# Router with stationary tokens, ranks by differences, and a transposed first gather, in a fused attention and mixture-of-experts block

## Chip, core and metric

One core of a Trainium2 chip. The metric is the device time of one execution in microseconds (us). Engines are named as the profile names them: PE (TensorE, with PEld for its weight loads), DVE (VectorE), ACT (ScalarE), POOL (GpSimd) and SP (SyncE, which here only issues DMAs). All data is 32-bit floating point unless said otherwise.

## What is computed

256 tokens of width 2048 pass a block with a spatial gating unit and a forgetting attention side by side, and then a mixture of 32 experts, of which each token uses two. Cut to the part that matters here:

```python
x = x + (g_sgu * y_sgu + g_fox * y_fox) @ w_out          # end of the first half
h2 = rms_norm(x, norm2_g)
g_logits = h2 @ w_rg + b_rg                              # 4 groups
e_logits = (h2 @ w_re + b_re).reshape(T, 4, 8)           # 8 experts in each
grp = argmax(g_logits); e_logits = e_logits[grp]         # one group a token
top_v, top_i = top_k(e_logits, 2)                        # two experts of it
w_top = softmax(top_v) * softmax(g_logits)[grp]
# each expert: y = (silu(xi @ w_g[e]) * (xi @ w_u[e])) @ w_d[e] on its tokens, added with the gate
```

## The kernel before

**First half.** The tokens lie as two blocks of 128 (`NT = 2`, index `tb`). Every product with a large weight goes through `half`: 8 k-tiles of weight come in by one DMA, ACT and DVE split them into a high and a low part (lines 237 and 238), and PE makes three products for each (lines 243 to 245). Between the k-tiles, `tick` runs steps of a queue of generators, `side`: small work of the chunk before is put into PE's order among the large products. The last chunks are the product with `w_out`, in five column ranges: three of 512 and two of 256.

**Router.** After each column range, `out_side` adds the result to `x1`, takes the squares for the norm (into `ss`), transposes `x1` by 128 x 128 pieces (line 646), copies two k-tiles out of PSUM with the norm weight `g2T` multiplied in (line 648), and multiplies with the router weight `wr` (line 655). There the weight is stationary (64 columns) and 256 tokens move; even and odd k-tiles gather in the two halves of the partitions of one tile, `r_ps`. After the last range `r_ps` is copied to SBUF by ACT, and two products with `fold` (two identities one over the other) add the halves and turn the result to tokens by 36 logits (`l_ps`, line 699). Line 706 scales by the norm and adds the bias. Then DVE finds the group (`first_max`), the eight logits of that group, and each expert's rank among the eight by comparing all pairs (lines 749 to 776). PE keeps busy meanwhile with `keep_warm(WARM[5])`, 60 small products that nobody reads. Five small products count each expert's tokens (`c_ps`), and `pos1` gives each token its slot.

**Experts.** An expert has 32 slots (`CAP`). `gather` picks its tokens from `x1` by products with a selection matrix `sel` (line 826: `sel` stationary, 512 columns of `x1` moving, four ranges side by side in the array), copies them (line 829), transposes (line 832) and scales by `g2p` (line 834) to `xT`. `hidden` multiplies `xT` with the gate or up weight (line 873); `silu`, `times_up` and `down` follow. While one expert is worked on, the next one's tokens are gathered.

**Expert weights** come in loads of 2 MB (12 MB for an expert) into tiles that are free by then: `order` and `free` give tiles to loads in turn, and line 561 issues them on SP's queue. Eleven tiles' worth are filled before the experts start: the last of these, `rb` and the second `mT`, may be overwritten only when the last product with `w_out` is done. After them no tile is free until the first expert's gate product has read the first one, `hT`.

The order on each engine is fixed when the program is built.

Of the kernel before, what the change touches and what calls it, by code (L numbers as in the profile page):

```python
# [9 lines left out]
F32 = mybir.dt.float32  # L10
# [4 lines left out]
ALU = mybir.AluOpType  # L15
AX = mybir.AxisListType

P = 128
# [15 lines left out]
HW = 2 * QW  # L34
CUTS = (0, 2, 4, 6, 8, 12, 16)
AHEADS = (2, 1, 1, 0, 1, 0, 1, 0, 0, 1, 0, 1, 1)
FRONT = ("g1T", "g2T", "wr", "fold", "br", "qkg", "bsT", "bfr", "mhalf", "eps_t", "ss", "rstd")
WARM = (45, 20, 0, 6, 4, 60, 0)
OVER_AT = 1
NEG = -1.0e30  # L40

# [2 lines left out]
def hybrid_block(ctx: ExitStack, tc: tile.TileContext, a, out, dbg=None):  # L44
# [11 lines left out]
    def ctile(shape, dt, name):  # L56
        return (fc if name in FRONT else cp).tile(shape, dt, tag=name, name=name)

# [2 lines left out]
    g2T = ctile([P, KT], F32, "g2T")  # L61
    g2p = ctile([P, 4, 4], F32, "g2p")
    wr = ctile([P, KT, 64], F32, "wr")
    fold = ctile([P, NG + NE], F32, "fold")
    br = ctile([P, NG + NE], F32, "br")
    qkg = ctile([P, 2], F32, "qkg")
    bsT = ctile([P, NH], F32, "bsT")
# [434 lines left out]
    zz = z_chunk(9)  # L502
    flush()
    load_small([(g2T, "g2T"), (wr, "wr"), (br, "br"), (g2p, "g2p")])
    side.append(evac_act(zz, va, AF.Copy, 512))
    side.append(attention_side(qT, kT, va))

# [116 lines left out]
        side.append(m_side(y2, t, n))  # L624

    r_ps = scp.tile([P, 512], F32, tag="sc", name="r_ps")[:, :S]

    def out_side(zz, b, c0, width):  # L630
        nk = width // P
        k0 = c0 // P
        for tb in range(NT):
            xs = x1[:, tb, c0:c0 + width]
            nc.vector.tensor_tensor(xs, xs, zz[tb], ALU.add)
        yield
        for tb in range(NT):
            xs = x1[:, tb, c0:c0 + width]
            sq = zt_tile()[:, :width]
            keep(nc.scalar.activation(sq, xs, AF.Square, accum_out=ss[:, tb, b:b + 1]))  # L640
        xTs = []
        for i in range(0, nk, 2):
            ps = tr_tile().rearrange("p (i t) q -> p i t q", i=2)
            for j in range(2):
                for tb in range(NT):
                    keep(nc.tensor.transpose(ps[:, j, tb], x1[:, tb, c0 + (i + j) * P:c0 + (i + j + 1) * P], ident))
            xT = zt_tile().rearrange("p (i t) -> p i t", i=2)
            nc.vector.tensor_tensor(xT, ps.rearrange("p i t q -> p i (t q)"),
                                    g2T[:, k0 + i:k0 + i + 2].unsqueeze(2).to_broadcast([P, 2, S]), ALU.mult)
            xTs.append(xT)  # L650
            yield
        for i, xT in enumerate(xTs):
            for j in range(2):
                kt = k0 + 2 * i + j
                keep(nc.tensor.matmul(r_ps[64 * j:64 * j + 64], wr[:, kt], xT[:, j], start=(kt < 2), stop=(kt >= KT - 2)))
            yield

    def w_out(c0, width, k):
# [28 lines left out]
    for z, b, c0 in parts:  # L687
        load(AHEADS[b + 8])
        half(z, w_out(c0, 256, 1), mT[1], start=False, width=256)
        flush()  # L690
        side.append(out_side(z, b, c0, 256))
    room([rings[used["ring"] % 2].rearrange("p a b -> p (a b)")])
    load(2)
    flush()
    rT = zt_tile()[:, :S]
    nc.scalar.activation(rT, r_ps, AF.Copy)
    l_ps = scp.tile([P, 512], F32, tag="sc", name="l_ps")[:, :NT * (NG + NE)].rearrange("p (t e) -> p t e", t=NT)
    for tb in range(NT):
        nc.tensor.matmul(l_ps[:, tb], rT[:, tb * P:(tb + 1) * P], fold, start=True, stop=True)
    s2 = small.tile([P, NT], F32, tag="s2", name="s2")  # L700
    nc.vector.tensor_reduce(s2, ss[:, :, :4], AX.X, ALU.add)
    nc.vector.tensor_scalar(s2, s2, 1.0 / D, EPS, ALU.mult, ALU.add)
    nc.vector.scalar_tensor_tensor(s2, ss[:, :, 4], 1.0 / D, s2, ALU.mult, ALU.add)
    rsqrt(rstd2, s2)
    for tb in range(NT):
        nc.vector.scalar_tensor_tensor(lg[:, tb], l_ps[:, tb], rstd2[:, tb:tb + 1], br, ALU.mult, ALU.add)
    front.close()
    if dbg is not None:
        nc.sync.dma_start(dbg[:, 0:2 * D], x1.rearrange("p a b -> p (a b)"))
# [23 lines left out]
    tt, ts, stt = nc.vector.tensor_tensor, nc.vector.tensor_scalar, nc.vector.scalar_tensor_tensor  # L733
    red = nc.vector.tensor_reduce

    def first_max(v, n, name):

        mx = rt([P, NT], name + "m")
        red(mx, v, AX.X, ALU.max)
        k = rt([P, NT, n], name + "k")  # L740
        tt(k, v, over(mx, n), ALU.is_equal)
        tt(k, k, desc[:, EPG - n:].unsqueeze(1).to_broadcast([P, NT, n]), ALU.mult)
        km = rt([P, NT], name + "km")
        red(km, k, AX.X, ALU.max)
        oh = rt([P, NT, n], name + "oh")
        tt(oh, k, over(km, n), ALU.is_equal)
        return mx, oh

    gl = lg[:, :, 0:NG]
    gm, goh = first_max(gl, NG, "g")  # L750
    gd = rt([P, NT, NG], "gd")
    tt(gd, gl, over(gm, NG), ALU.subtract)
    nc.scalar.activation(gd, gd, AF.Exp)
    pick = rt([P, NT, NG, EPG], "pick")
    goh4 = goh.unsqueeze(3).to_broadcast([P, NT, NG, EPG])
    tt(pick, lg[:, :, NG:].rearrange("p t (g e) -> p t g e", g=NG), goh4, ALU.mult)
    e8 = rt([P, NT, EPG], "e8")
    red(e8, pick.rearrange("p t g e -> p t e g"), AX.X, ALU.add)

    sq4 = [P, NT, EPG, EPG]  # L760
    bt = mo.tile(sq4, F32, tag="th", name="bt")
    be = mo.tile(sq4, F32, tag="h", name="be")
    ei = e8.unsqueeze(3).to_broadcast(sq4)
    ej = e8.unsqueeze(2).to_broadcast(sq4)
    tt(be, ej, ei, ALU.is_equal)
    tt(bt, ej, ei, ALU.is_gt)
    tt(be, be, low.unsqueeze(1).to_broadcast(sq4), ALU.mult)
    tt(bt, bt, be, ALU.add)
    rank = rt([P, NT, EPG], "rank")
    red(rank, bt, AX.X, ALU.add)  # L770
    oh12 = rt([P, NT, EPG], "oh12")
    ts(oh12, rank, 1.0, None, ALU.is_le)
    oo = rt([P, NT, NE], "oo")
    ob = rt([P, NT, NE], "ob", BF16)
    for o in (ob, oo):
        tt(o.rearrange("p t (g e) -> p t g e", g=NG), goh4, oh12.unsqueeze(2).to_broadcast([P, NT, NG, EPG]), ALU.mult)

    keep_warm(WARM[5])
    c_ps = scm.tile([P, 512], F32, tag="sc", name="c_ps")
# [12 lines left out]
    def gates():  # L792

        oh1 = rt([P, NT, EPG], "oh1")
        oh2 = rt([P, NT, EPG], "oh2")
        ts(oh1, rank, 0.0, None, ALU.is_equal)
        ts(oh2, rank, 1.0, None, ALU.is_equal)
        w1 = rt([P, NT], "w1")
        w2 = rt([P, NT], "w2")
        gs = rt([P, NT], "gs")  # L800
        red(gs, gd, AX.X, ALU.add)
        md = rt([P, NT, EPG], "md")
        tt(md, oh2, oh1, ALU.subtract)
        tt(md, md, e8, ALU.mult)
        red(w2, md, AX.X, ALU.add)
        nc.scalar.activation(w2, w2, AF.Exp)
        ts(w1, w2, 1.0, None, ALU.add)
        tt(w1, w1, gs, ALU.mult)
        nc.vector.reciprocal(w1, w1)
        tt(w2, w2, w1, ALU.mult)  # L810
        for tb in range(NT):
            ts(oh1[:, tb], oh1[:, tb], w1[:, tb:tb + 1], None, ALU.mult)
            stt(oh1[:, tb], oh2[:, tb], w2[:, tb:tb + 1], oh1[:, tb], ALU.mult, ALU.add)
        tt(gw.rearrange("p t (g e) -> p t g e", g=NG), goh4, oh1.unsqueeze(2).to_broadcast([P, NT, NG, EPG]), ALU.mult)
        nc.vector.tensor_copy(cnt, c_ps[:, 2 * NE:3 * NE])

    def gather(e, sel=None):

        if sel is None:
            sel = mo.tile([P, NT, CAP], F32, tag="sel", name="sel", bufs=2)  # L820
            for tb in range(NT):
                ts(sel[:, tb], iota1, pos1[:, tb, e:e + 1], rstd2[:, tb:tb + 1], ALU.is_equal, ALU.mult)  # L822
        x_ps = xgp.tile([P, 512], F32, tag="xg", name="x_ps")
        for tb in range(NT):
            for c in range(4):
                nc.tensor.matmul(x_ps[32 * c:32 * c + 32], sel[:, tb], x1[:, tb, c * 512:(c + 1) * 512],  # L826
                                 start=(tb == 0), stop=(tb == NT - 1))
        xg = mo.tile([P, 512], F32, tag="xg", name="xg")
        nc.scalar.activation(xg, x_ps, AF.Copy)
        t_ps = xgp.tile([P, 4, SL], F32, tag="xg", name="t_ps")  # L830
        for i in range(4):
            nc.tensor.transpose(t_ps[:, i], xg[:, i::4], ident)
        xT = mo.tile([P, 4, 4, CAP], F32, tag="xT", name="xT", bufs=2)
        tt(xT, t_ps.rearrange("p i (c s) -> p i c s", c=4), g2p.unsqueeze(3).to_broadcast([P, 4, 4, CAP]), ALU.mult)
        return xT

    def turned(eq, tag, dt=F32):
# [182 lines left out]
            nc.tensor.matmul(ps, gt[:, tb * P:(tb + 1) * P], y[:, cs], start=True, stop=True)  # L1020
            tt(acc[tb][:, cs], x1[:, tb, cs] if q == 0 else acc[tb][:, cs], ps, ALU.add)

    nxt = gather(0)

    four = rt([P, CAP], "four")
    red(four, ident.rearrange("p (j c) -> p c j", j=4), AX.X, ALU.add)
# [124 lines left out]
```

## Time and profile before

| | |
|---|---|
| median of 3 runs | 1547.36 us (1546.90 to 1548.42) |
| the profiled execution | 1546.67 us, its span 1545.0 us |
| PE, DVE, ACT, POOL busy | 85%, 38%, 27%, 2% of the span |
| DMA, slices 1 to 16 of 40 | 146 to 383 GB/s |
| DMA, slices 18 to 39 | 425 to 429 GB/s |

The first 620 us are the first half of the block, in which PE is always busy. The rest is the experts, in which the DMA engines are always busy. The router lies between the two.

### The profile page before, as it was taken

What the parts mean: (1) busy time and instruction counts of PE and PEld (TensorE: products, weight loads), DVE (VectorE), ACT (ScalarE), POOL (GpSimd) and SP (SyncE); (2) the same over time, 40 slices, a digit from 0 to 9 for tenths busy, and PEclk for the clock granted to TensorE, in tenths of its full rate; (3) what the DMA queues carried; (4) which work ended last, traced back from release to release, by engine and by line L of the source; (5) the groups of instructions that cost most, each with busy time, mean ns of one, the idle gap of its engine ahead of it and who ended that gap; (6) DMA issues with size and microseconds to landing.
All of it is one profiled execution on the core that took longest, in us unless ns stands there. A gap on an engine that the chain in (4) does not pass through costs nothing.

```text
span 1545.0 us, 18399 instructions
## 1 busy us (share of the span) xinstructions
PE 1309.3 (85%) x7472; PEld 741.7 (48%) x7472; DVE 586.4 (38%) x1126; ACT 410.6 (27%) x753; POOL 31.9 (2%) x38
## 2 busy tenths in 40 slices
PE   9999999999999999898667768768768767867758
PEld 8788888888888878433222223212212212212213
DVE  6766766666665655322113112112112112112114
ACT  6645455545555444111100010010010000100001
POOL 0300100000000000000000000000000000000000
PEclk9999999999999999999989788889878889889899
DMA  9554453354546865899999999999999999999998
GB/s 383 234 209 171 167 208 146 148 214 184 220 174 251 346 245 194 351 426 426 427 425 426 425 429 427 427 426 427 426 426 427 427 427 427 426 427 427 426 427 328
DMA packets 48455, 523.53 MB, mean 339 GB/s; under 512 B 5872, under 2 KB 10608, under 8 KB 14448
## 3 DMA queue, kind: packets, MB, share of 16 engines
q1 hardware_dynamic: 47072, 520.22, 81.6%
q10 hardware_dynamic: 1296, 2.11, 0.5%
q8 instruction: 60, 0.98, 0.3%
q14 instruction: 27, 0.22, 0.0%
HBM read 520.21 MB, written 2.10 MB: 338 GB/s over the span
## 4 chain that ended last, share of the span: by engine, by line
DMA 51%; PE 45%; DVE 2%; ACT 1%; issue 1%; POOL 0%; SPq 0%; DVEq 0%; ACTq 0%
DMA so<-in_we_d_dram 12%; DMA ex<-in_we_d_dram 12%; PE z L243 12%; PE z L244 12%; PE z L245 12%; DMA rb<-in_we_g_dram 9%; DMA w<-in_we_u_dram 9%; DMA hT<-in_we_g_dram 9%; PE ps L873 3%; PE ps L1020 1%; PE y_ps L908 1%; PE x_ps L826 1%; DVE wl L238 1%; PE s_ps L884 1%; ACT wh L237 0%
## 5 line engine op out<-in xcount | busy, mean ns | idle before, releaser
L238 DVE TENSOR_TENSOR wl<-w,wh 128x512 fp32r<-128x512 f32 x220 | 151.0, 690 | 110.7 <-ACT wh L237 110.4
L237 ACT ACTIVATE wh<-w 128x512 fp32r<-128x512 f32 x220 | 138.0, 631 | 152.3 <-PE z L245 76.7
L243 PE MATMUL z<-wh,hT 128*128 128x512 f32 x382 | 151.6, 398 | 0.2 <-ACT wh L237 0.2
L244 PE MATMUL z<-wl,hT 128*128 128x512 f32 x382 | 149.4, 391 | 2.6 <-DVE wl L238 2.5
L245 PE MATMUL z<-wh,hT 128*128 128x512 f32 x382 | 149.1, 390 | 0.0
L881 ACT ACTIVATE q<-ps 128x256 f32<-128x256 f32 x64 | 24.5, 383 | 462.2 <-PE ps L873 459.5
L882 DVE COPY q<-ps 128x256 f32<-128x256 f32 x64 | 27.1, 424 | 273.1 <-ACT q L881 273.1
L917 DVE COPY mT<-y_ps 32x512 f32<-32x512 f32 x62 | 42.4, 684 | 201.2 <-PE y_ps L908 180.9
L915 ACT ACTIVATE mT<-y_ps 32x512 f32<-32x512 f32 x62 | 36.5, 589 | 290.5 <-DVE mT L917 290.4
L884 PEld LDWEIGHTS s_ps<-four,q 128*128 128x128 f32 x512 | 64.8, 195 | 98.9 <-ACT q L881 96.2
L884 PE MATMUL s_ps<-four,q 128*128 128x32 f32 x512 | 72.1, 284 | 32.5 <-ACT q L881 32.5
L873 PE MATMUL ps<-w,xT 128*32 128x512 f32 x512 | 76.0, 674 | 24.8 <-DMA w<-in_we_g_dram 18.7
L873 PE MATMUL ps<-hT,xT 128*32 128x512 f32 x512 | 81.7, 725 | 17.9 <-DMA hT<-in_we_g_dram 14.1
L826 PE MATMUL x_ps<-x,sel 128*32 128x512 f32 x512 | 84.4, 656 | 0.7 <-DVE sel L822 0.7
L873 PE MATMUL ps<-so,xT 128*32 128x512 f32 x352 | 64.4, 818 | 19.6 <-DMA so<-in_we_g_dram 19.5
L244 PEld LDWEIGHTS z<-wl,hT 128*128 128x128 f32 x382 | 71.8, 188 | 18.6 <-DVE wl L238 4.7
L243 PEld LDWEIGHTS z<-wh,hT 128*128 128x128 f32 x382 | 71.7, 188 | 15.3 <-issue 0.8
L245 PEld LDWEIGHTS z<-wh,hT 128*128 128x128 f32 x382 | 71.7, 188 | 15.1
L243 PE MATMUL z<-ex,hT 128*128 128x512 f32 x194 | 76.1, 393 | 0.0
L244 PE MATMUL z<-ex,hT 128*128 128x512 f32 x194 | 75.6, 390 | 0.0
L245 PE MATMUL z<-ex,hT 128*128 128x512 f32 x194 | 75.6, 390 | 0.0
L238 DVE TENSOR_TENSOR wl<-third,wh 128x512 fp32r<-128x512 f32 x75 | 59.4, 801 | 34.1 <-ACT wh L237 34.1
(303 smaller groups left out, 1825.8 us busy)
## 6 DMA issues: line engine op xcount, KB each, us to landing
w<-in_we_u_dram SPq DMA_DIRECT2D x21, 2048.0 KB, 34.3
w<-in_w_in_dram SPq DMA_DIRECT2D x20, 2048.0 KB, 7.3
hT<-in_we_u_dram SPq DMA_DIRECT2D x20, 2048.0 KB, 34.3
so<-in_we_d_dram SPq DMA_DIRECT2D x20, 2048.0 KB, 35.0
third<-in_w_in_dram SPq DMA_DIRECT2D x14, 2048.0 KB, 7.4
hT<-in_we_g_dram SPq DMA_DIRECT2D x12, 2048.0 KB, 34.3
so<-in_we_u_dram SPq DMA_DIRECT2D x12, 2048.0 KB, 36.7
w<-in_we_g_dram SPq DMA_DIRECT2D x11, 2048.0 KB, 34.3
```

The lines of the kernel that those rows point to most:

```text
L237: nc.scalar.activation(wh, wv, AF.Copy)
L238: nc.vector.tensor_tensor(wl, wv, wh.bitcast(F32), ALU.subtract)
L243: nc.tensor.matmul(z[tb], hi, wh[:, i - j], start=first, stop=False)
L244: nc.tensor.matmul(z[tb], hi, wl[:, i - j], start=False, stop=False)
L245: nc.tensor.matmul(z[tb], lo, wh[:, i - j], start=False, stop=final)
L826: nc.tensor.matmul(x_ps[32 * c:32 * c + 32], sel[:, tb], x1[:, tb, c * 512:(c + 1) * 512], start=(tb == 0), stop=(tb == NT - 1))
L873: nc.tensor.matmul(ps[32 * i:32 * i + 32], xT[:, i, c], w[:, i], start=(c == 0), stop=(c == 3))
L881: nc.scalar.activation(q[:, 0:256], ps[:, 0:256], AF.Copy)
L882: nc.vector.tensor_copy(q[:, 256:], ps[:, 256:])
L884: nc.tensor.matmul(o[:, j * CAP:(j + 1) * CAP], q[:, j * P:(j + 1) * P], four, start=True, stop=True)
L915: nc.scalar.activation(o, i, AF.Copy)
L917: nc.vector.tensor_copy(o, i)
```

## The change

- The router product (`l_ps`) keeps 128 tokens stationary and moves the router weight's 36 columns: for each k-tile two products, one for each token block, into two accumulators. `r_ps`, its copy and `fold` go. `g2T` is multiplied into `wr` once, by POOL, after the weight is loaded; `out_side` copies without it, in the last range half on DVE and half on ACT.
- The ranks of groups and experts come from one function, `ranks`, on differences; `first_max` goes. What only the gates need (`gm`, `gd`) moves to `gates`.
- The first expert's gather, `gather_first`, makes the transposed tokens directly: 128 columns of `x1`, every fourth one, are stationary and `sel` moves (32 columns), in four blocks of eight products, each scaled by DVE on its own.
- `WARM[5]` is 45 in place of 60.

```diff
-WARM = (45, 20, 0, 6, 4, 60, 0)
+WARM = (45, 20, 0, 6, 4, 45, 0)
...
     load_small([(g2T, "g2T"), (wr, "wr"), (br, "br"), (g2p, "g2p")])
+    nc.gpsimd.tensor_tensor(wr, wr, g2T.unsqueeze(2).to_broadcast([P, KT, 64]), ALU.mult)
...
-            nc.vector.tensor_tensor(xT, ps.rearrange("p i t q -> p i (t q)"),
-                                    g2T[:, k0 + i:k0 + i + 2].unsqueeze(2).to_broadcast([P, 2, S]), ALU.mult)
+            if b < 4:
+                nc.vector.tensor_copy(xT, pv)
+            else:
+                keep(nc.vector.scalar_tensor_tensor(s2, ss[:, :, 4], 1.0 / D, s2, ALU.mult, ALU.add))
+                keep(nc.vector.tensor_copy(xT[:, 0], pv[:, 0]))
+                nc.scalar.activation(xT[:, 1], pv[:, 1], AF.Copy)
...
-                keep(nc.tensor.matmul(r_ps[64 * j:64 * j + 64], wr[:, kt], xT[:, j], start=(kt < 2), stop=(kt >= KT - 2)))
+                for tb in range(NT):
+                    keep(nc.tensor.matmul(l_ps[tb], xT[:, j, tb * P:(tb + 1) * P], wr[:, kt, 0:NG + NE],
+                                          start=(kt == 0), stop=(kt == KT - 1)))
...
-    nc.scalar.activation(rT, r_ps, AF.Copy)
-    for tb in range(NT):
-        nc.tensor.matmul(l_ps[:, tb], rT[:, tb * P:(tb + 1) * P], fold, start=True, stop=True)
...
+    def ranks(v, n, name, ta, tb_):
+        sq = [P, NT, n, n]
+        d = mo.tile(sq, F32, tag=ta, name=name + "d")
+        r = mo.tile(sq, F32, tag=tb_, name=name + "r")
+        tt(d, v.unsqueeze(2).to_broadcast(sq), v.unsqueeze(3).to_broadcast(sq), ALU.subtract)
+        for tb in range(NT):
+            stt(r[:, tb], d[:, tb], 0.0, low[:, 0:n, 0:n], ALU.is_equal, ALU.mult)
+        stt(r, d, 0.0, r, ALU.is_gt, ALU.add)
+        rank = rt([P, NT, n], name)
+        red(rank, r, AX.X, ALU.add)
+        return rank
...
+    def gather_first():
+        sel = mo.tile([P, NT, CAP], F32, tag="sel", name="sel", bufs=2)
+        for tb in range(NT):
+            ts(sel[:, tb], iota1, pos1[:, tb, 0:1], rstd2[:, tb:tb + 1], ALU.is_equal, ALU.mult)
+        xT = mo.tile([P, 4, 4, CAP], F32, tag="xT", name="xT", bufs=2)
+        for c in range(4):
+            t_ps = xgp.tile([P, 512], F32, tag="xg", name="t_ps")[:, :P].rearrange("p (i s) -> p i s", i=4)
+            for i in range(4):
+                for tb in range(NT):
+                    nc.tensor.matmul(t_ps[:, i], x1[:, tb, c * 512 + i:(c + 1) * 512:4], sel[:, tb],
+                                     start=(tb == 0), stop=(tb == NT - 1))
+            tt(xT[:, :, c], t_ps, g2p[:, :, c:c + 1].to_broadcast([P, 4, CAP]), ALU.mult)
+        return xT
...
-    nxt = gather(0)
+    nxt = gather_first()
```

In the order of the built program a 32-bit product counts once; in the trace it is two instructions with a weight load each. Here is PE from the last counting product to the first expert's gate and up products, before (names: `hT` and `so` are weight tiles, `x_67` is `x1`, `q` the hidden rows):

```order
L784 MATMUL c_ps<-ob,onesb 128x32
L826 MATMUL x_ps<-x_67,sel 32x512 x8
L832 MATMUL t_ps<-ident,xg 128x128 x4
L826 MATMUL x_ps<-x_67,sel 32x512 x5
L873 MATMUL ps<-hT_4182,xT 32x512 x8
L873 MATMUL ps<-hT_4183,xT 32x512 x8
L873 MATMUL ps<-so_4270,xT 32x512
```

and the same place in the changed program:

```order
L774 MATMUL c_ps<-ob,onesb 128x32
L842 MATMUL t_ps<-sel,x_67 128x32 x32
L883 MATMUL ps<-hT_4181,xT 32x512 x8
L883 MATMUL ps<-hT_4182,xT 32x512 x8
L883 MATMUL ps<-so_4269,xT 32x512
L894 MATMUL s_ps<-four,q 128x32 x4
L883 MATMUL ps<-so_4269,xT 32x512 x7
```

Thirty-two small products stand where twelve stood, all of them ahead of the first gate product, and the five products of the second expert's gather have left the gap (they now follow the up product).

PE again, at the last but one router step among the products with `w_out`, before:

```order
L244 MATMUL z<-wl,mT_2684 128x256
L655 MATMUL r_ps<-zt,wr 64x256 x2
L245 MATMUL z<-wh,mT_2684 128x256
L243 MATMUL z<-wh,mT_2684 128x256
L244 MATMUL z<-wl,mT_2684 128x256
```

and changed:

```order
L242 MATMUL z<-wl,mT_2683 128x256
L659 MATMUL l_ps<-wr,zt 128x36 x4
L243 MATMUL z<-wh,mT_2683 128x256
L241 MATMUL z<-wh,mT_2683 128x256
L242 MATMUL z<-wl,mT_2683 128x256
```

Nothing else moved here; two products became four. There are eight such steps, of which seven stand ahead of the last product with `w_out`.

## Rows read from the trace of the kernel before

**Rows 1.** The page: the chain that ended last, by engine.

```profile
DMA 51%; PE 45%; DVE 2%; ACT 1%; issue 1%; POOL 0%; SPq 0%; DVEq 0%; ACTq 0%
```

**Rows 2.** Stretches: busy us (and instructions) by engine, clock, DMA share, GB/s.

```profile
637.00:638.00 1.00, 1.00 (x15) 0.26 (x8) 0.00 (x0) 0.00 (x0) 0.00 (x0) 1.00 0.00 0
...
640.00:690.00 50.00, 46.77 (x353) 17.41 (x355) 12.01 (x30) 7.28 (x16) 0.00 (x0) 1.00 1.00 425
...
1250.00:1500.00 250.00, 178.56 (x1152) 58.70 (x1144) 45.74 (x94) 23.20 (x52) 1.80 (x1) 0.88 1.01 427
```

**Rows 3.** SP's queue from 622 us: start, us, and the load issued.

```profile
622.88 0.43 SPq L561 DMA_DIRECT2D mT<-in_we_d_dram  x1
...
638.36 0.33 SPq L561 DMA_DIRECT2D hT<-in_we_d_dram  x1
...
654.09 0.33 SPq L561 DMA_DIRECT2D third<-in_we_u_dram  x1
```

**Rows 4.** PE in order of time round one router step.

```profile
617.94 0.28 PE L243 MATMUL z<-wh,mT 128*128 128x256 f32 x1
618.06 0.28 PE L244 MATMUL z<-wl,mT 128*128 128x256 f32 x1
618.27 0.65 PE L655 MATMUL r_ps<-zt,wr 128*64 128x256 f32 x4
618.85 0.38 PE L245 MATMUL z<-wh,mT 128*128 128x256 f32 x1
```

**Rows 5.** In order of time: the last router copy, the logits, and a half-sized copy.

```profile
623.56 0.69 DVE L648 TENSOR_TENSOR zt<-ps,g2T 128x512 f32<-128x512 f32 x1 [0.64 <-PE ps L646]
...
626.12 0.42 DVE L706 SCALAR_TENSOR_TENSOR lg<-l_ps,rstd,br 128x36 f32<-128x36 f32 x2 [0.44 <-PE l_ps L699]
...
640.55 0.42 DVE L882 COPY q<-ps 128x256 f32<-128x256 f32 x1 [5.10 <-ACT q L881]
```

**Rows 6.** First step of the choice of experts, and the first counting product.

```profile
626.64 0.16 DVE L739 TENSOR_REDUCE gm<-lg 128x2 f32<-128x8 f32 x1
...
630.36 0.18 PE L780 MATMUL c_ps<-ob,striub 128*128 128x32 bf16 x1 [0.93 <-issue]
```

**Rows 7.** The first gather's first products, and the first gate products.

```profile
631.33 1.92 PE L826 MATMUL x_ps<-x,sel 128*32 128x512 f32 x16 [0.70 <-DVE sel L822]
...
635.54 0.63 PE L873 MATMUL ps<-hT,xT 128*32 128x512 f32 x3
```

**Rows 8.** Weight loads of 128 columns, and the clock round the third row.

```profile
633.97 0.56 PEld L832 LDWEIGHTS t_ps<-ident,xg 128*128 128x128 f32 x4 [1.62 <-ACT xg L829]
...
640.78 0.97 PEld L884 LDWEIGHTS s_ps<-four,q 128*128 128x128 f32 x8 [0.84 <-ACT q L881]
...
926.34 1.78 PEld L884 LDWEIGHTS s_ps<-four,q 128*128 128x128 f32 x8 [2.28 <-ACT q L881]
...
924.00:934.00 10.00, 8.60 (x44) 3.20 (x40) 0.71 (x2) 1.15 (x3) 0.00 (x0) 0.50 1.00 421
```

**Rows 9.** PE round a fall of its clock, and the idle-time products of the router.

```profile
625.91 3.52 PE L165 MATMUL ps<-onesb 128*128 128x128 bf16 x60
...
656.42 1.90 PE L873 MATMUL ps<-w,xT 128*32 128x512 f32 x16
...
693.80 2.30 PE L873 MATMUL ps<-rb,xT 128*32 128x512 f32 x16
696.65 1.09 PE L884 MATMUL s_ps<-four,q 128*128 128x32 f32 x8 [0.55 <-ACT q L881]
...
699.02 3.42 PE L873 MATMUL ps<-hT,xT 128*32 128x512 f32 x16
...
698.68:702.08 3.40, 3.40 (x17) 0.71 (x17) 0.00 (x0) 0.00 (x0) 0.00 (x0) 0.50 1.02 434
```

**Rows 10.** POOL on a tile of 128 x 1024, and a stretch beside it.

```profile
64.09 2.83 POOL L316 TENSOR_TENSOR v_sb<-v_sb,lng 128x1024 f32<-128x1024 f32 x1
...
66.00:68.00 2.00, 0.87 (x4) 0.43 (x3) 2.00 (x2) 0.63 (x1) 1.92 (x2) 1.00 0.00 0
```

More of the change, by code (lines that the diff above doesn't have):

```diff
@@ L36 @@
 AHEADS = (2, 1, 1, 0, 1, 0, 1, 0, 0, 1, 0, 1, 1)
-FRONT = ("g1T", "g2T", "wr", "fold", "br", "qkg", "bsT", "bfr", "mhalf", "eps_t", "ss", "rstd")
-WARM = (45, 20, 0, 6, 4, 60, 0)
+FRONT = ("g1T", "g2T", "wr", "br", "qkg", "bsT", "bfr", "mhalf", "eps_t", "ss", "rstd")
+WARM = (45, 20, 0, 6, 4, 45, 0)
 OVER_AT = 1
@@ L63, in hybrid_block @@
     wr = ctile([P, KT, 64], F32, "wr")
-    fold = ctile([P, NG + NE], F32, "fold")
     br = ctile([P, NG + NE], F32, "br")
@@ L624, in hybrid_block @@
         side.append(m_side(y2, t, n))
-    r_ps = scp.tile([P, 512], F32, tag="sc", name="r_ps")[:, :S]
+    l_ps = [scp.tile([P, 512], F32, tag="sc", name="l_ps")[:, :NG + NE] for _ in range(NT)]
     def out_side(zz, b, c0, width):
@@ L647, in out_side @@
             xT = zt_tile().rearrange("p (i t) -> p i t", i=2)
-            nc.vector.tensor_tensor(xT, ps.rearrange("p i t q -> p i (t q)"),
-                                    g2T[:, k0 + i:k0 + i + 2].unsqueeze(2).to_broadcast([P, 2, S]), ALU.mult)
+            pv = ps.rearrange("p i t q -> p i (t q)")
+            if b < 4:
[4 more added lines that the diff above has]
+                nc.scalar.activation(xT[:, 1], pv[:, 1], AF.Copy)
             xTs.append(xT)
@@ L690, in hybrid_block @@
         flush()
+        if b == 4:
+            s2 = small.tile([P, NT], F32, tag="s2", name="s2")
+            nc.vector.tensor_reduce(s2, ss[:, :, :4], AX.X, ALU.add)
+            nc.vector.tensor_scalar(s2, s2, 1.0 / D, EPS, ALU.mult, ALU.add)
         side.append(out_side(z, b, c0, 256))
@@ L694, in hybrid_block @@
     flush()
-    rT = zt_tile()[:, :S]
-    nc.scalar.activation(rT, r_ps, AF.Copy)
-    l_ps = scp.tile([P, 512], F32, tag="sc", name="l_ps")[:, :NT * (NG + NE)].rearrange("p (t e) -> p t e", t=NT)
-    for tb in range(NT):
-        nc.tensor.matmul(l_ps[:, tb], rT[:, tb * P:(tb + 1) * P], fold, start=True, stop=True)
[L700 to L703, printed above, removed]
     rsqrt(rstd2, s2)
     for tb in range(NT):
-        nc.vector.scalar_tensor_tensor(lg[:, tb], l_ps[:, tb], rstd2[:, tb:tb + 1], br, ALU.mult, ALU.add)
+        nc.vector.scalar_tensor_tensor(lg[:, tb], l_ps[tb], rstd2[:, tb:tb + 1], br, ALU.mult, ALU.add)
     front.close()
@@ L749, in hybrid_block @@
     gl = lg[:, :, 0:NG]
[L750 to L753, printed above, removed]
+    le = lg[:, :, NG:].rearrange("p t (g e) -> p t g e", g=NG)
+    grank = ranks(gl, NG, "grank", "gk", "gkr")
     pick = rt([P, NT, NG, EPG], "pick")
-    goh4 = goh.unsqueeze(3).to_broadcast([P, NT, NG, EPG])
-    tt(pick, lg[:, :, NG:].rearrange("p t (g e) -> p t g e", g=NG), goh4, ALU.mult)
+    for tb in range(NT):
+        stt(pick[:, tb], grank[:, tb].unsqueeze(2).to_broadcast([P, NG, EPG]), 0.0, le[:, tb], ALU.is_equal, ALU.mult)
@@ L757, in hybrid_block @@
     e8 = rt([P, NT, EPG], "e8")
     red(e8, pick.rearrange("p t g e -> p t e g"), AX.X, ALU.add)
[L760 to L769, printed above, removed]
@@ L770, in hybrid_block @@
-    red(rank, bt, AX.X, ALU.add)
-    oh12 = rt([P, NT, EPG], "oh12")
-    ts(oh12, rank, 1.0, None, ALU.is_le)
+    goh = rt([P, NT, NG], "goh")
+    ts(goh, grank, 0.0, None, ALU.is_equal)
+    goh4 = goh.unsqueeze(3).to_broadcast([P, NT, NG, EPG])
+    rank = ranks(e8, EPG, "rank", "th", "h")
     oo = rt([P, NT, NE], "oo")
@@ L775, in hybrid_block @@
     for o in (ob, oo):
-        tt(o.rearrange("p t (g e) -> p t g e", g=NG), goh4, oh12.unsqueeze(2).to_broadcast([P, NT, NG, EPG]), ALU.mult)
+        for tb in range(NT):
+            stt(o[:, tb].rearrange("p (g e) -> p g e", g=NG), rank[:, tb].unsqueeze(1).to_broadcast([P, NG, EPG]), 1.0,
+                goh4[:, tb], ALU.is_le, ALU.mult)
     keep_warm(WARM[5])
@@ L797, in gates @@
         ts(oh2, rank, 1.0, None, ALU.is_equal)
+        gm = rt([P, NT], "gm")
+        gd = rt([P, NT, NG], "gd")
+        red(gm, gl, AX.X, ALU.max)
+        tt(gd, gl, over(gm, NG), ALU.subtract)
+        nc.scalar.activation(gd, gd, AF.Exp)
         w1 = rt([P, NT], "w1")
@@ L834, in gather @@
         tt(xT, t_ps.rearrange("p i (c s) -> p i c s", c=4), g2p.unsqueeze(3).to_broadcast([P, 4, 4, CAP]), ALU.mult)
+        return xT
+    def gather_first():
+        sel = mo.tile([P, NT, CAP], F32, tag="sel", name="sel", bufs=2)
+        for tb in range(NT):
+            ts(sel[:, tb], iota1, pos1[:, tb, 0:1], rstd2[:, tb:tb + 1], ALU.is_equal, ALU.mult)
[3 more added lines that the diff above has]
+            for i in range(4):
+                for tb in range(NT):
+                    nc.tensor.matmul(t_ps[:, i], x1[:, tb, c * 512 + i:(c + 1) * 512:4], sel[:, tb],
+                                     start=(tb == 0), stop=(tb == NT - 1))
+            tt(xT[:, :, c], t_ps, g2p[:, :, c:c + 1].to_broadcast([P, 4, CAP]), ALU.mult)
         return xT
```

12 lines of the change are left out of this document (removed).

## Prediction

> **What bounds the kernel now.** I read the page first: the chain that ended last is half DMA, half PE [rows 1]. The table of stretches tells where each holds. In the first half PE has no idle time; from 640 us to the end the DMA engines have none, at 425 to 427 GB/s, whatever PE and its clock do [rows 2]. Between the two lies the router, and there the DMA engines stand still: at 637 us they move nothing [rows 2]. SP's queue says why: the last load that could go out early was issued at 622.88, the next at 638.36, when the first gate product had read `hT` [rows 3]. From there on loads are always in the queue (between the issues at 638.36 and 654.09 four loads of 2 MB went out, some 20 us of transfer at 425 GB/s for 15.7 us of time, so nearly 4 us in hand). So one instant decides the total: the release of `hT`. A microsecond that it comes later is a microsecond at the end. It is reached by a single chain: last product with `w_out`, router, choice of experts, first gather, first half of the gate product.
>
> **Router steps.** Seven of the eight steps stand among the `w_out` products, where PE is the bound. One costs 0.79 us from the product before to the product after, where large products follow each other at 0.12: 0.67 us for four instructions [rows 4]. After the change a step has eight, each with a weight load of 128 columns. The nearest row is the eight loads of `s_ps`, with 32 moving columns: 0.97 us, 0.12 each [rows 8]. So +0.30 a step, **+2.1 us** for seven. Ends: 0, if some loads hide behind the large products; +3.1, if a load takes the 0.14 of the row of four [rows 8].
>
> **From the last product to the logits.** Copy, four products, ACT's copy, four products and scaling take 623.56 to 626.54, 2.98 us [rows 5]. After: a small DVE step ahead of the copy (0.1), the copy of half the size (0.42 by the DVE row of that size [rows 5]; ACT's half runs beside it), eight products (0.97 for the loads and 0.1 for the last to end), the scaling (0.42) and two hand-overs of 0.06: 2.13 us, so −0.85.
>
> **Ranks.** From the first step to the first counting product pass 3.72 us [rows 6], thirteen steps that wait for each other. Now there are ten, four of which are pairs, and the fill-in work (`four`, `thr`, `gm`, `gd`) still stands between them in the order. I take −0.25, with ends +0.2 and −0.6. `gm` and `gd` are needed only by the gates. The chain in all: **−1.1 us**, ends −0.6 and −1.5.
>
> **The first gather.** Now: 631.33 to 635.54 to the first gate product, 2.82 more to the release of `hT`, of which four leftover products of the second gather take 0.43; 7.03 in all [rows 7, 3]. After: 64 instructions, each with its own load of 128 columns, and all of them ahead of the first gate product in PE's order. DVE's four scalings run beside them; the first gate products need only the first block. At 0.12 a load the gather takes 7.7 us (7.0 to 9.0 at 0.11, as one load's tail is in the row of eight, and at 0.14, a row whose columns are also taken every fourth). With 2.4 for half the gate product that is 10.1, **+3.1 us**. ACT's copy and the transposes, which go, were cheaper than what comes.
>
> **The clock.** The products that DVE's chain is covered with last 3.52 us for 60, 0.059 each [rows 9]; 45 last 2.65 and end some 0.9 us earlier. From there to the gather's first product about 2.7 us go by with five tiny products in them. Then comes the gather: 32 moving columns behind each load of 128, so products fill a small part of the time. In the trace the granted clock fell from 2.4 to 1.2 GHz after just such work: full products ended at 696.1, eight `s_ps` products and a transpose followed, and 2.6 us later the clock was 0.50 [rows 9]. At 1.2 GHz eight loads take 1.78 us in place of 0.97 [rows 8], 0.20 to 0.22 each, and 16 gate products 3.42 in place of 1.90 [rows 9]. I think it will fall here. When, I can't read: by the 2.6 us as early as the gather's first product, by a later start as late as 3 us into it. I take 1.5: 12 loads at 0.12, 52 at 0.21, 12.4 us. The gate products then start at the low clock and I give them 3.9 in place of 2.4. That is 16.3 against 7.03: **+9.3 us**.
>
> **At nothing.** POOL's product of `g2T` into `wr` stands hundreds of us ahead of its use, in the first half, but POOL on such a tile slows DVE: two of its 0.7 us steps filled 2 us, and PE was idle for 1.1 us of them after several such tiles in a row [rows 10]. For one tile the splits in hand cover it; uncovered it costs up to 1.1 us. Behind it in POOL's queue nothing is due for long. SP's wait for the overflow count moves behind seven more loads; it stood ahead of the load at 638.36 and did not hold it.
>
> **The sum.** 9.3 − 1.1 + 2.1 = +10.3 us on the profiled 1546.67 (1545.0 and 1.67 around it): 1557.0. The median of the runs is 0.69 above that execution, so **1557.7 us**. The case's own ends: clock falling 3 us in with gate products at the full clock, best chain, free steps: 26 × 0.11 + 38 × 0.20 + 2.4 − 7.03 − 1.5 = +4.3, 1551.7; falling at the first product, 64 × 0.22 + 4.1 − 7.03 − 0.6 + 3.1 = +13.7, 1561.
>
> **Rivals.** *The clock holds.* The gather has no pause of PE, and the sparse 1.9 us ahead of the first gather now (629.43 to 631.33 [rows 9, 7]) are followed by products at full speed (16 in 1.92 us). Then +3.1 − 1.1 + 2.1 = +4.1: 1551.5 us, with ends +0.9 (7.0 + 2.4 − 7.03 − 1.5) and +6.9, 1548.3 to 1554.3. The Trainium skill, TensorE: Matmul & The Clock Gate, section "Why this matters for your kernels", asks that PE have no idle gaps between bursts of matmuls; by that rule taken at its word a gather without a gap keeps the clock and this rival's time would be right. The fall at 698.7 came after work with pauses in it, which agrees; no row has small products alone for as long as here.
>
> *Loads hide.* If PE loads the next weight while a product runs, here and in the router steps, down to the pitch of the covering products (0.059): gather 64 × 0.059 + 2.4 − 7.03 = −0.8; the last router step 8 × 0.06 less, chain −1.6; the others 0.47 in place of 0.67, −1.4. In all −3.8: 1543.6 us, faster. Each 0.01 of pitch is worth 1.3 us, so it decides below 0.088. Against it: eight loads in a row took 0.97, at 32-bit data like these; the 0.059 is of bf16. The Trainium skill, the same page, section "Back-to-back issue gap", gives 81 ns a matmul for a stream of weight loads and matmuls of 128 columns. By it, as an estimate, the sum would be −0.9, 1546.5, no change; the row of eight disagrees.
>
> *The gap costs nothing*, as the loads catch up: against it, they ran at 425 to 427 GB/s in every stretch to the end, so there is nothing to catch up with.
>
> **Chances.** Clock falls 0.72, holds 0.18, loads hide 0.10. A measurement of this kernel tells about 0.2%, 3.1 us, from no change. The first case is slower throughout; of the second 0.12 lies above +3.1 and 0.06 within; of the third 0.06 is faster and 0.04 within. So slower 0.84, same 0.10, faster 0.06. The range: the first case up to its high end without the rarest fall, and the second from 1550 on: 1550.0 to 1560.5, which leaves out about 2 in 10; the first alone is 1551.7 to 1561.
>
> **What would show it.** In the profile after: DMA still idle, for longer; the release of `hT` (issue of its second load) some 10 us later than 638.4, and later loads without a break; 64 loads of the gather in 12 us, at 0.12 first and 0.21 then, with the clock at 0.50 in the stretch; the last `w_out` product about 2 us later; the logits 0.85 us nearer to it; counting products 3.5 us after the logits. I am wrong if the gather's loads come closer than 0.1 us, if the clock stays 1.00 through it, if the gate products start before the gather ends, or if the loads have gaps after the release.

## The result, and the profile after

The changed kernel takes 1558.28 us (median of 4 runs, 1557.99 to 1558.67); the kernel before takes 1547.13 (4 runs, 1546.81 to 1548.42). The ratio is 1.0073, 95% interval 1.006 to 1.0086: slower by some 11 us, where 1557.7 was predicted. The profiled execution took 1557.99 us, 11.32 more than the one of before.

I read it in the order of the prediction. First the stretches of the trace after, columns as in [rows 2]:

```profile
636.75:649.50 12.75, 12.75 (x61) 10.14 (x64) 3.26 (x19) 0.00 (x0) 0.00 (x0) 0.51 0.01 2
651.00:701.00 50.00, 46.77 (x351) 17.20 (x349) 11.43 (x28) 7.30 (x16) 0.00 (x0) 1.00 1.00 424
1250.00:1500.00 250.00, 181.84 (x1140) 57.66 (x1132) 45.31 (x92) 23.00 (x51) 1.80 (x1) 0.85 1.01 427
```

For 12.75 us the DMA engines move next to nothing, and TensorE works without a pause at a clock of 0.51. Behind it the DMA engines have no idle time, as before. SP's queue, which answers to [rows 3]:

```profile
649.66 0.33 SPq L560 DMA_DIRECT2D hT<-in_we_d_dram  x1
...
666.25 0.33 SPq L560 DMA_DIRECT2D third<-in_we_u_dram  x1
```

The release of `hT` came at 649.66 in place of 638.36, 11.30 us later, against 11.32 in the time. That they agree to 0.02 is chance: the spans, 1545.0 and 1555.9 us, differ by 10.9, and from the release to the end of the execution the eleven traces of this case have 908.2 to 908.8 us in nine, 909.3 with more keep-warm products and 910.2 with both edits. To a few tenths of a microsecond the reading holds. Next TensorE, in order of time, from the first router step and the last one among the `w_out` products to the gate products ([rows 4, 6, 7, 9]):

```profile
553.12 0.39 PE L243 MATMUL z<-wh,mT 128*128 128x512 f32 x1
553.35 0.97 PE L659 MATMUL l_ps<-wr,zt 128*128 128x36 f32 x8
554.16 0.48 PE L241 MATMUL z<-wh,mT 128*128 128x512 f32 x1
...
618.68 0.28 PE L242 MATMUL z<-wl,mT 128*128 128x256 f32 x1
618.80 1.07 PE L659 MATMUL l_ps<-wr,zt 128*128 128x36 f32 x8
619.70 0.36 PE L243 MATMUL z<-wh,mT 128*128 128x256 f32 x1
...
623.01 0.28 PE L243 MATMUL z<-wh,mT 128*128 128x256 f32 x1
...
625.88 2.68 PE L164 MATMUL ps<-onesb 128*128 128x128 bf16 x45
629.99 0.18 PE L770 MATMUL c_ps<-ob,striub 128*128 128x32 bf16 x1 [1.43 <-issue]
...
646.08 5.22 PE L883 MATMUL ps<-hT,xT 128*32 128x512 f32 x32
```

The last product with `w_out` starts 0.82 us later than before, where it stands as

```profile
622.19 0.28 PE L245 MATMUL z<-wh,mT 128*128 128x256 f32 x1
```

The counting product stands at 629.99, 0.37 sooner than in [rows 6]. The gather starts at 631.01, 0.32 sooner than in [rows 7]. Up to here the change gains a little. The gather's 64 instructions then take 15.07 us to the first gate product, where 12.4 were predicted, and the gate product takes 3.58 more to the release. From gather to release that is 18.65 against 7.03, +11.62; less the 0.32, +11.30.

What makes the gather so long stands in one more view, the stretches on either side of the clock's fall, counting the gather's line alone (busy us and number of products, then of weight loads, clock, DMA share, GB/s):

```profile
631.00:632.26 1.26, 1.25 (x6) 1.25 (x6) 1.00 1.07 449
632.26:646.10 13.84, 13.84 (x60) 13.75 (x59) 0.50 0.17 70
```

The clock did fall, 1.25 us into the gather. But 59 loads in 13.75 us are 0.233 us each, and single loads ahead of the fall start at 631.216, 631.449, 631.683, 631.916 and 632.149: 0.233 apart too, at the full clock. The prediction gave the loads 0.12 there and 0.21 at the low clock. So the time came out right while its mechanism looks wrong, and the experiments ask two things: what sets 0.233, and what the clock costs.

### The profile page after: what moved, and what is told of

Same layout as the page of the kernel before. It is cut to its first block, busy times and chain, and to the rows that moved or that the text cites. A ratio compares the mean times of both kernels' runs of the same rounds, so it can differ in the third digit from the quotient of the medians.

```text
span 1555.9 us, 18521 instructions
## 1 busy us (share of the span) xinstructions
PE 1330.2 (85%) x7529; PEld 760.9 (49%) x7529; DVE 587.8 (38%) x1133; ACT 411.1 (26%) x752; POOL 33.6 (2%) x38
## 4 chain that ended last, share of the span: by engine, by line
DMA 50%; PE 46%; DVE 2%; ACT 1%; issue 1%; POOL 0%; SPq 0%; DVEq 0%; ACTq 0%
PE z L241 11%; PE z L242 11%; PE z L243 11%; DMA w<-in_we_u_dram 9%; DMA so<-in_we_d_dram 7%; DMA so<-in_we_g_dram 7%; DMA ex<-in_we_d_dram 5%; DMA third<-in_we_g_dram 5%; DMA hT<-in_we_u_dram 4%; DMA rb<-in_we_g_dram 4%; DMA hT<-in_we_g_dram 4%; PE ps L883 3%; DMA bm<-in_we_d_dram 2%; DMA hT<-in_we_d_dram 2%; PE y_ps L918 1%; PE t_ps L842 1%
## 5 line engine op out<-in xcount | busy, mean ns | idle before, releaser
L883 PE MATMUL ps<-w,xT 128*32 128x512 f32 x512 | 82.0, 702 | 23.7 <-DMA w<-in_we_g_dram 18.7
L883 PE MATMUL ps<-so,xT 128*32 128x512 f32 x352 | 60.7, 766 | 18.4 <-DMA so<-in_we_g_dram 15.6
L1030 PE MATMUL ps<-mT,gt 128*128 128x512 f32 x128 | 66.7, 648 | 6.8 <-DVE mT L927 6.5
```

The lines of the kernel that those rows point to most:

```text
L883: nc.tensor.matmul(ps[32 * i:32 * i + 32], xT[:, i, c], w[:, i], start=(c == 0), stop=(c == 3))
```

## The experiments

Each edit is against the changed kernel, but for the last two, which say so. Theory A is the prediction's: the clock sets the pitch of the loads. Theory B was formed from the rows above: the step of four columns does.

**The old gather back.**

```diff
-    nxt = gather_first()
+    nxt = gather(0)
```

> The changed kernel, with the gather of before for the first expert; the router, the ranks and the 45 keep-warm products stay changed. If the whole loss sits in the new gather (my reading): the gather starts 0.32 us sooner than before (631.01 against 631.33) and takes its 7.03 us again, so the release of hT moves from 638.36 to about 638.0 and the time is 1546.8 us, 0.02% under before. If the shorter keep-warm stretch is what lets the clock fall, it falls here too: the 512-wide products of the gather at half clock take up to twice their 3 us or so, and the time is 1550 to 1554 us.

Measured: 1547.40 us (11 runs) beside 1546.89 of before on the same chip (15 runs), ratio 1.0002, interval 0.9992 to 1.0013. In its trace the last product, the counting product and the gather stand within 0.1 us of the changed kernel's:

```profile
623.10 0.28 PE L243 MATMUL z<-wh,mT 128*128 128x256 f32 x1
...
630.09 0.18 PE L770 MATMUL c_ps<-ob,striub 128*128 128x32 bf16 x1 [1.44 <-issue]
...
631.11 1.92 PE L821 MATMUL x_ps<-x,sel 128*32 128x512 f32 x16 [0.71 <-DVE sel L817]
633.75 0.75 PE L827 MATMUL t_ps<-ident,xg 128*128 128x128 f32 x4 [0.72 <-ACT xg L824]
```

The release is at 638.13, and the clock holds through the gather with 45 products as with 60. So the whole loss sits in the new gather, and the rest of the change is worth nothing that can be measured.

**Columns side by side.** This takes away the step alone.

```diff
-                    nc.tensor.matmul(t_ps[:, i], x1[:, tb, c * 512 + i:(c + 1) * 512:4], sel[:, tb],
+                    nc.tensor.matmul(t_ps[:, i], x1[:, tb, c * 512 + i * P:c * 512 + (i + 1) * P], sel[:, tb],
```

> Here gather_first loads 128 columns that lie side by side instead of every fourth one, so expert 0 sees its tokens' columns in another order; nothing else differs. In the trace of the changed kernel the loads start 0.233 us apart already in the 1.25 us before the recorded clock falls, and 0.233 us apart after it. Theory A (the clock sets the pitch, as predicted): side by side or not, 11 loads at 0.111 and 53 at 0.2135 make 12.5 us where 15.0 were, time about 1555.8 us. Theory B (the step of four columns doubles a load of a 32-bit product, at either clock): pitch 0.111 to the end if the clock holds, gather 7.1 us, time about 1550.3 us less up to 1.7 us if the gate products run at full clock too. If the clock falls and the pitch is then 0.2135, theory A holds for contiguous loads and B for strided ones, and the time is that of A.

Measured: 1556.73 us, ratio to before 1.0064, interval 1.0049 to 1.008. The same view as above, of this kernel:

```profile
631.60:634.23 2.63, 2.58 (x23) 2.58 (x24) 1.00 1.08 458
636.00:642.50 6.50, 6.50 (x32) 6.50 (x32) 0.50 0.02 6
```

At the full clock the single starts are 0.112 us apart, at the low one 0.213. The gather took 11.47 us, the release came at 646.82. So side by side theory A holds: loads follow the clock. With the step of four they were 0.233 at either clock, and theory B holds there. The last case of the expectation is what came; the gather is a microsecond shorter than its 12.5 because the clock fell 2.58 us into it in place of 1.25.

**More columns behind each load.** This is to hold the clock, with the step kept.

```diff
-                                     x1[:, tb, c * 512 + i:(c + 1) * 512:4], sel[:, tb],
+                                     x1[:, tb, c * 512 + i:(c + 1) * 512:4], sel[:, tb].unsqueeze(1).to_broadcast([P, 4, CAP]),
...
-            tt(xT[:, :, c], t_ps, g2p[
+            tt(xT[:, :, c], t_ps[:, :, 0:CAP], g2p[
```

> Each of the 64 loads is followed by 128 moving columns instead of 32: the 32 columns of sel taken four times over, three copies of the result not used. Theory A (the clock fell because so little was done behind each load, and the fallen clock set the pitch): the clock stays up, loads come every 0.12 us, the gather takes 7.8 us and the gate products 1.9, time about 1549.4 us. Theory B (strided load of 0.233 us whatever the clock): the gather keeps its 14.9 us; with the clock up only the gate products gain, 1.7 us, time 1556.6 us; with the clock down 1558.3 us.

Measured: 1556.60 us, ratio 1.0059, interval 1.0044 to 1.0075. The gather's line on either side of 634.71, where the clock rose again:

```profile
631.60:634.71 3.11, 3.07 (x13) 3.07 (x14) 0.50 1.02 435
634.71:646.70 11.99, 11.99 (x53) 11.94 (x52) 1.00 0.06 23
```

Here most of the gather has the full clock, and it still takes 15.13 us: 52 loads in 11.94 us are 0.23 each. The gate products behind it and the release:

```profile
646.77 3.64 PE L883 MATMUL ps<-hT,xT 128*32 128x512 f32 x32
648.76 0.33 SPq L560 DMA_DIRECT2D hT<-in_we_d_dram  x1
```

From the first gate product to the release pass 1.99 us in place of 3.58. So for these loads the clock costs nothing, and for the gate products behind them 1.6 us. Theory B's 1556.6 is what came in the median; the execution of this trace took 1557.24, and its gather started 0.63 us later than the changed kernel's.

**More keep-warm products ahead of the gather.**

```diff
-WARM = (45, 20, 0, 6, 4, 45, 0)
+WARM = (45, 20, 0, 6, 4, 69, 10)
```

> The changed kernel with 69 keep-warm products ahead of the ranks' product instead of 45, and 10 more between it and the gather, so that TensorE works from 625.9 to the gather's start with hardly a gap. Theory A (clock): the fall comes later than 1.25 us into the gather; each us that it comes later saves about 4 loads at 0.21 instead of 0.12, so with 2 us later about 1 us less, time 1557.3 us or below. Theory B (strided load): nothing, 1558.3 us, whenever the clock falls. If the keep-warm products reach past the ranks' result, they delay the gather by at most 0.5 us.

Measured: 1560.00 us, ratio 1.0088, interval 1.0071 to 1.0106. The clock fell at 633.37, 1.55 us into the gather in place of 1.25, and the gather took the same 15.07. So the fall came 0.3 us later, too little for the time to tell A from B; what speaks for B is the pitch, 0.233 ahead of the fall as behind it. The cover was not what was meant, either: the pause of 1.43 us ahead of the counting products went, but the one ahead of the gather grew from 0.71 to 1.11. The gather started 1.99 us after the counting product, in place of 1.02. VectorE's step that reads the counts (`pos`) began at 631.17 and not at 630.34:

```profile
631.09 0.17 DVE L802 TENSOR_SCALAR w<-w 128x2 f32<-128x2 f32 x1 [0.27 <-ACT w L801]
631.17 0.22 DVE L776 SCALAR_TENSOR_TENSOR pos<-c_ps,oo 128x64 f32<-128x64 f32 x1
```

In this program `pos` stands on VectorE behind four steps of the gates (lines 798 to 802), which follow it in the changed kernel, and the last of them waited for ScalarE. So the delay came with another order on VectorE. Whether the ten products, which had ended at 630.71, held `pos` as well is not shown. The release came at 650.59, 0.93 us later than in the changed kernel; the rest of the 1.7 us lies behind it and stays open.

**Both edits at once**, side by side and 128 columns behind each load.

> Both edits at once: columns side by side (expert 0 sees them in another order) and 128 moving columns behind each load. If the two causes add up (the step of four columns doubles the pitch of the loads at either clock; the fallen clock costs the contiguous loads 0.21 instead of 0.11 and the gate products about 1.7 us), the gather takes 64 x 0.111 to 0.12 = 7.1 to 7.8 us, the clock stays up, the release of hT comes 9.0 to 9.7 us sooner than in the changed kernel, and the time is 1548.6 to 1549.3 us. If instead the clock falls whenever loads come this densely, whatever is behind them, the loads go back to 0.2135 and the time is that of side-by-side columns alone, 1555 to 1557 us.

Measured: 1550.34 us (10 runs, 1548.72 to 1552.45), ratio 1.0014, interval 1.0004 to 1.0024. The gather's line over the clock's three stretches:

```profile
631.20:632.37 1.17, 1.08 (x9) 1.08 (x10) 1.00 1.06 441
632.37:635.78 3.41, 3.41 (x18) 3.41 (x17) 0.50 0.75 320
635.78:640.00 4.22, 4.22 (x40) 4.22 (x39) 1.00 0.02 8
```

The two causes add up, but for a stretch: the clock fell even with 128 columns behind each load, and came back within the gather. In that stretch 17 loads passed where some 30 would have at 0.112, which is 1.5 us. The gather took 8.97 us and the release came at 642.24, 7.4 us sooner than in the changed kernel where 9.0 to 9.7 were expected; the 1.5 us are most of what is missing. The trace is of the slowest of the ten executions, 1552.45 us: 5.5 less than the changed kernel's, where the release came 7.4 sooner. Part of the difference can be seen near the end, in products that wait for a load, first here, then in the changed kernel:

```profile
1510.50 3.64 PE L918 MATMUL y_ps<-so,h 128*32 128x512 f32 x16 [1.76 <-DMA so<-in_we_d_dram]
...
1517.65 1.92 PE L918 MATMUL y_ps<-so,h 128*32 128x512 f32 x16 [1.54 <-DMA so<-in_we_d_dram]
```

They ran at a clock of 0.50 here and of 1.00 there; how much of the total this makes was not tried. Even without the step and mostly at the full clock, the 64 loads take 8.97 us, where the old gather's 16 products with four transposes reach the gate products in 4.21.

**Four steps in one gather.** The quarters take every eighth, every fourth, every second column, and neighbours, again with 128 columns behind each load.

```diff
-                    nc.tensor.matmul(t_ps[:, i], x1[:, tb, c * 512 + i:(c + 1) * 512:4], sel[:, tb],
+                    nc.tensor.matmul(t_ps[:, i], x1[:, tb, i:i + P * (8 >> c):8 >> c], sel[:, tb].unsqueeze(1).to_broadcast([P, 4, CAP]),
```

> A look at the pitch of the loads alone: of the gather's four quarters the first takes every eighth column, the second every fourth, the third every second, the last columns side by side, each with 128 moving columns behind every load so that the clock stays up (expert 0 gets other columns than it should). Theory B1 (a threshold: rows of 16 bytes and more apart cost double): 0.233, 0.233, 0.11 to 0.12, 0.11 us. Theory B2 (cost in proportion to the stretch that is read): 0.47, 0.233, 0.12 to 0.17, 0.11 us. Theory A (no cost of the step, all was the clock): 0.11 to 0.12 us in all four.

The gather's line, a stretch for each quarter of 16 loads (a load at the edge is counted on both sides):

```profile
631.10:635.00 3.90, 3.88 (x16) 3.88 (x17) 1.00 0.94 397
635.00:638.70 3.70, 3.70 (x17) 3.70 (x18) 1.00 0.04 16
638.70:640.60 1.90, 1.90 (x17) 1.90 (x18) 1.00 0.00 0
640.60:642.40 1.80, 1.80 (x18) 1.80 (x17) 1.00 0.00 0
```

From start to start: 0.238, 0.233, 0.117 to 0.120 and 0.112 us, all at the full clock. A step of two columns costs 5 to 7%, four doubles the pitch, eight adds 2% more. So there is a threshold (B1) between two and four columns, three was not tried, and no price in proportion to the stretch. That the clock stayed up is not shown to come from the 128 columns: in this trace it had fallen earlier, from 626.14 to 629.55, during the keep-warm products. Its one run took 1553.37 us.

**A product in place of a transpose.** The old gather, with its four transposes of every fourth column written as products.

```diff
-            nc.tensor.transpose(t_ps[:, i], xg[:, i::4], ident)
+            nc.tensor.matmul(t_ps[:, i], xg[:, i::4], ident, start=True, stop=True)
```

> The changed kernel with the old gather, whose four transposes of every fourth column are written as products with the identity. The transposes' loads come every 0.12 us although they take every fourth column too, which speaks against the step as the cause. If it is the kind of load (a 32-bit product, two instructions, each with a load) that the step doubles, 8 loads of 0.233 us make 1.9 us where 4 transposes made 0.5, the release of hT comes 1.4 us later than with transposes (638.13), and the time is 1548.3 us or so. If the step costs products nothing and it is something else about x1's columns, 8 loads of 0.12 make 1.0 us, 0.5 us later.

```profile
633.73 2.13 PE L827 MATMUL t_ps<-ident,xg 128*128 128x128 f32 x8 [0.72 <-ACT xg L824]
...
636.68 0.63 PE L883 MATMUL ps<-hT,xT 128*32 128x512 f32 x3
```

Same columns, same tile, same clock: the four transposes took 0.75 us (the row of the old gather above), the eight instructions of the products 2.13, 0.233 from start to start where the transposes have 0.12. The release came at 639.50, 1.37 later, and the one run took 1547.77 us. So it is the load of a 32-bit product that the step doubles, and a transpose's load does not show it. Why the two differ stays open.

**The router undone**: the kernel before with the new ranks and 45 keep-warm products alone.

```diff
-WARM = (45, 20, 0, 6, 4, 60, 0)
+WARM = (45, 20, 0, 6, 4, 45, 0)
...
-    def first_max(v, n, name):
+    def ranks(v, n, name, ta, tb_):
...
```

> Before with the new ranks and 45 keep-warm products alone: old router with its stationary weights, old gather. My term for the router's steps was +2.1 us on the last product of w_out; the traces with the new router have that product at 622.85 to 623.65 us, 623.25 in the mean, the one trace without it at 622.19. If the router costs 1.1 us there, this trace has it at 622.0 to 622.5; if it was the execution that differed, at 622.9 to 623.6. From there to the logits it should be 3.94 us to the start of lg's row as before (2.93 with the new router), from the logits to the ranks' product 0.27 less than before. Time within 0.1% of before, 1546.6 us.

Measured: 1546.73 us (10 runs), ratio 0.9996, interval 0.9986 to 1.0007. Its first router step, its last and the last product:

```profile
553.18 0.40 PE L245 MATMUL z<-wh,mT 128*128 128x512 f32 x1
553.50 0.65 PE L655 MATMUL r_ps<-zt,wr 128*64 128x256 f32 x4
554.09 0.50 PE L243 MATMUL z<-wh,mT 128*128 128x512 f32 x1
...
622.23 0.28 PE L245 MATMUL z<-wh,mT 128*128 128x256 f32 x1
...
630.32 0.18 PE L770 MATMUL c_ps<-ob,striub 128*128 128x32 bf16 x1
```

From the product ahead of the first router step to the last product it is 69.05 us here; with the new router 69.89 (553.12 to 623.01) and 69.91 (553.19 to 623.10, old gather back). So the new router's steps cost 0.84 to 0.86 us. The 1.1 in my expectation was too much: two of the traces behind it had reached the first router step 0.6 us late. The ranks from their first step (626.88 here) to the counting product: 3.44 us, where [rows 6] have 3.72. From the last product to the logits it is 4.13, 0.19 more than expected: the clock was at 0.50 from 625.8 to 629.2 in this trace, and the last products with `fold` fell into that.

**The old gather's copies split**, on the kernel with the router undone, for the first expert alone.

```diff
-        nc.scalar.activation(xg, x_ps, AF.Copy)
+            nc.scalar.activation(xg[:, 0:256], x_ps[:, 0:256], AF.Copy)
+            nc.vector.tensor_copy(xg[:, 256:], x_ps[:, 256:])
...
-        tt(xT, t_ps.rearrange("p i (c s) -> p i c s", c=4), g2p.unsqueeze(3).to_broadcast([P, 4, 4, CAP]), ALU.mult)
+        for cs in ((slice(0, 4),) if e else (slice(0, 1), slice(1, 4))):
+            n = cs.stop - cs.start
+            tt(xT[:, :, cs], t_ps.rearrange("p i (c s) -> p i c s", c=4)[:, :, cs], ...
```

> An attempt at a version better than both: before with the new ranks (as in the run with the router undone), and for the first expert alone the old gather's two copies cut: the 128x512 copy of x_ps between ScalarE and VectorE (0.60 us on ScalarE alone), and the scaling into xT first for the quarter that the first gate products read, then for the rest. If both copies stand on the chain as the trace shows, the release of hT comes 0.4 to 0.7 us sooner than 638.36, and the time is 0.4 to 0.7 us, 0.03 to 0.05%, under before: 1546.1 us beside 1546.7, too little for the comparison to tell. If VectorE's half queues behind its other work, nothing, or up to 0.3 us later.

Measured: 1547.46 us (11 runs) beside 1546.75, ratio 1.0005, interval 0.9996 to 1.0015. The copies, the transposes, the first gate products and the release:

```profile
633.26 0.38 ACT L827 ACTIVATE xg<-x_ps 128x256 f32<-128x256 f32 x1 [1.14 <-PE x_ps L821]
...
633.68 0.42 DVE L828 COPY xg<-x_ps 128x256 f32<-128x256 f32 x1
...
634.16 0.75 PE L831 MATMUL t_ps<-ident,xg 128*128 128x128 f32 x4 [0.96 <-DVE xg L828]
634.84 1.04 PE L821 MATMUL x_ps<-x,sel 128*32 128x512 f32 x2
635.30 4.02 PE L890 MATMUL ps<-hT,xT 128*32 128x512 f32 x32
...
637.68 0.33 SPq L561 DMA_DIRECT2D hT<-in_we_d_dram  x1
```

The release came 0.68 us sooner, but the first cut has no part in it. VectorE's half queued, 0.42 behind ScalarE's, and the transposes start 2.89 us into the gather (which starts at 631.27) in place of 2.65. From the transposes to the gate products it is 1.14 in place of 1.56, and from there to the release 2.38 in place of 2.82 [rows 7, 8, 3]. But the edit also changed the order on TensorE: two instructions of the second gather stand ahead of the gate products where nine stood, and none among the first of them. What the second cut earned apart from that order was not tried. The runs can't tell it: one by one they lie between 1545.77 and 1549.28. No version here beats the kernel before by what can be measured.

## Why the prediction was right, and where it was not

**The bound** was right. The release of `hT` moved by 11.30 and the time by 11.32, the DMA loads had no break behind it, and the old gather alone brought it all back. That the gap costs nothing is refuted.

**The first gather** was the step that failed in its reason. The prediction priced a load at 0.12 at the full clock, from eight loads of neighbouring columns and from four loads of every fourth column [rows 8]. The second row was that of transposes. For products with that step the price is 0.233, as the four steps and the product in place of the transpose showed. At the full clock throughout, side by side, the gather would by these rows have come to an estimated 64 × 0.112 plus 0.14 for the last product and its scaling, 7.3 us, and 1.98 to the release (2.4 was taken): +2.3 on 7.03, near the +3.1 predicted. The step of four adds 64 × 0.122 = 7.8. The fallen clock adds 1.6, all of it in the gate products.

**The clock** fell, 1.25 us into the gather where 1.5 was taken, and the gate products took 3.58 where 3.9 was given. But its share of the prediction's +9.3 was 6.2, and it cost 1.6. It had stood in for the step by a coincidence of size: 0.21, the load at the low clock, is near 0.233. So the forecast of the gather came out 2.3 us short, and not the 6.9 that the clock's true price would have left (3.1 + 1.6 against 11.6).

**The clock holds** as a rival is refuted, and its price with it: had the clock held, the time would have been about 1556.6, as the run with 128 columns shows, and not 1551.5. By the Trainium skill, TensorE: Matmul & The Clock Gate, section "Why this matters for your kernels", a matmul engine that leaves no idle gaps between bursts is spared the drop; taken at its word, this gather should have been. The trace disagrees: 12.75 us busy of 12.75 at a clock of 0.51. The prediction took the fall at 698.7 as agreeing with the rule. It doesn't bear it out either: the pauses ahead of that fall were 0.55 and 0.86 us, shorter than those that this section of the Trainium skill speaks of.

**Loads hide** is refuted in the gather: no pitch under 0.11 was seen within it but between its first loads (0.108). In the router steps some of it is true. **Router steps** were mis-sized: +2.1 predicted, +0.84 measured. One of the first six costs 1.04 or 0.93 us in place of 0.91 or 0.79, +0.13 to 0.14 each; the seventh has 1.02 in place of 0.79. Of each of the first six the products next to it give back 0.02 to 0.05, so that the seven come to 0.84 and not to 1.0. The first of a step's eight loads runs beside the large product before it: its load starts at 553.119, with that product, and the first two products start at 553.349 and 553.380, 0.03 apart, the others 0.11.

**From the last product to the logits** −0.85 was predicted and −0.92 came (3.93 to 3.01). **Ranks**: −0.25 predicted, −0.27 measured in the changed kernel (626.54 to 629.99) and −0.28 with the router undone. **At nothing** was put POOL's product, and rightly: the product ahead of the first router step starts at 553.12 in the changed kernel's trace and at 553.13 in the one of before.

**The sum**: 0.8 − 1.1 + 11.6 = +11.3, where 2.1 − 1.1 + 9.3 = +10.3 was predicted. Two errors of opposite sign, −1.3 in the router and +2.3 in the gather, left one microsecond. So that the time came so near is in part luck: of the 11.6 us of the largest term, 7.8 have a cause that the prediction didn't name.

## What to carry to other kernels

Take the price of a weight load from a row of the same operation, type and column step: a transpose is no model for a product, and a total that fits doesn't show that its terms do. Ahead of a critical path, count loads before columns: 64 loads with 32 columns behind each lost to 16 wide products, four transposes and two copies even with the step removed. And look at single starts on either side of a clock change before the clock is blamed.

## What was not expected of the hardware

- Loads of 128 columns for 32-bit products came every 0.112 us from neighbouring columns, 0.117 to 0.12 with a step of two (8 bytes), 0.233 with four (16 bytes) and 0.238 with eight. By the Trainium skill, Advanced Engine Details and Errata, section "SBUF Cachelines", a line is 16 bytes and accesses that each fall into another line pay a penalty, with a tolerance that depends on the type. The products agree with it, as their threshold lies above 8 bytes and not above 16; the transposes, 0.12 at a step of 16 bytes, do not show it. That the lines are the cause was not tried further.
- With the step of four the pitch was 0.233 at a clock of 1.00 and of 0.50 alike, so what limits these loads does not follow TensorE's clock; neighbouring columns went from 0.112 to 0.213.
- The clock fell in loads without a pause in the changed kernel, side by side, with more keep-warm products, and with both edits. With 128 columns behind each load it was back at 1.00 within the gather (at 634.71 and 635.78); with 32 it stayed at 0.50 to the gather's end, in all three traces. In the last four runs told above it fell during the keep-warm products and was back ahead of the gather, so none of them shows what holds it. Why it was at 0.50 already at the gather's first load in the run with 128 columns and the step of four stays open.
